# A stick-breaking and differential attention encoder on one core: the order of work in the first gate/up chunk, and two weights' rests moved to GpSimd

## The chip, the cores and the metric

The kernel runs on one core of a Trainium2 chip. The time is that of one execution on the device, in microseconds. A core has engines with a queue of instructions each, which run in order and wait for each other through semaphores: TensorE (PE in the profile, its weight loads PEld), VectorE (DVE), ScalarE (ACT), GpSimd (POOL) and SyncE (SP), whose queue here issues most of the transfers from the device's memory. GpSimd's queue issues transfers as well, here those that add to what they find (accumulating transfers). SBUF is the memory that the engines work in, PSUM the memory that TensorE writes its sums to.

## The reference

Two layers over 256 tokens of width 2048, all in float32. A layer is attention (eight stick-breaking heads, eight differential heads), a projection, a residual sum with a normalization, and a SwiGLU block with another:

```python
def swiglu(h, w_gate, w_up, w_down):
    return (jax.nn.silu(h @ w_gate) * (h @ w_up)) @ w_down

for l in range(DEPTH):                 # 2 layers
    h = rms_norm(x, pre_mix_norm[l])
    m = hybrid_mixer(h, l, ...)        # attention and the projection w_o
    x = x + rms_norm(m, post_mix_norm[l])
    h = rms_norm(x, pre_ffn_norm[l])
    f = swiglu(h, w_gate[l], w_up[l], w_down[l])   # 2048 -> 5632 -> 2048
    x = x + rms_norm(f, post_ffn_norm[l])
```

The change concerns the place where `x + rms_norm(m, ...)` ends and `h @ w_gate`, `h @ w_up` begin.

## The kernel before

**Products in three parts.** A float32 operand w is split into a rounded part `hi` (ScalarE copies w into TensorE's format) and a rest `lo` = w - hi (a subtraction on VectorE, 128x1024 elements for one weight pair). A product of x and w is then three products on TensorE: x's rest by hi, x's rounded part by hi, x's rounded part by lo. Each weight pair goes through four steps: its load (SP), `hi` (ScalarE), `lo` (VectorE), the products. `weights(i, ahead)` sees to it that the pairs up to i + ahead are prepared; `raw`, the buffer of a load, is one of four, so a load waits for the `lo` of the pair four places earlier (L241); `hi` and `lo` have six buffers each.

**Chunks.** The gate and up products run over chunks of 512 columns (`c`), each over eight pairs of 128 rows (`kp`). A pair is either done by `eight` (L1245: 24 products of 128x512, for two tokens' halves, gate and up), or by `seven` (L1127 to L1129: 21 products in place of 24), which needs sums: token sums `f` and `s`, split into `sh` and `sl` (`pair_sums`, `token_sums`, L1361, L1134 to L1145), and weight sums G and T. T is loaded (L257), then GpSimd's queue adds half of the gate weight to it with an accumulating transfer (L258), and `mixed_weights` makes from G and T the pieces `hi`, `lo` (L281), T's difference (L290), G's sum with it (L291) and their splits `Th`, `Tl` (L279, L281). In the first chunk the order of the pairs is `FIRST_ORDER` = 0, 1, 3, 2, 7, 4, 6, 5: four pairs (`first` to `fourth`) ahead of the loop, then 7 by `eight`, 4 and 6 by `seven`, 5 by `eight`. In layer 1 their weights have the numbers 128/129, 130/131, 132/133, 134/135, 136/137, 138/139, 140/141 and 142/143; in layer 2 each is 392 higher.

**The stretch around the change** (from L1252). x is updated column group by column group: `rescaled` (L647, VectorE, x + r * mg), then `turned_x` transposes four 128x128 blocks on TensorE (L502), `rounded_x` makes x's rounded part on ScalarE (L508) and `rest_of_x` its rest on VectorE (L516); `columns` is the last two together. TensorE meanwhile works on the pairs whose columns are there already. A part of this stretch is written out by hand (`tc.manual_schedule` for ScalarE, VectorE and TensorE): in it the instructions of an engine stand in the order of the source. Behind it the order is a scheduler's, which `tc.issue_after` can hold back: the instruction is placed after the named one. `rounded_next` gives the next pair's `hi` and returns a function that issues its `lo`; its argument is the engine, VectorE if none is given (L334). Before, the pairs 132 and 133 use it in this stretch; 134 to 137 come through `feed` (L317), as `eight(..., third, ...)` has the usual look-ahead of four.

**The squares.** The norm in front of the SwiGLU needs the mean of x squared: `inv_rms` (L542) has eight squares of 128x512 on ScalarE in each layer, then small steps on VectorE (L545, L485, L495, L496) and ScalarE (L483, L484). Its result is first used at the end of the chunk (L1413).

**Helped rests.** In later chunks two of the gate weights' rests are made by GpSimd (L310), one of them held back until the chunk before has its last seven-product pair's products.

Of the kernel before, what the change touches and what calls it, by code (L numbers as in the profile page):

```python
# [13 lines left out]
ALU = mybir.AluOpType  # L14
# [7 lines left out]
NT = S // P  # L22
# [22 lines left out]
FIRST_ORDER = (0, 1, 3, 2, 7, 4, 6, 5)  # L45
# [7 lines left out]
AFTER = mybir.DependencyInfo(mybir.DependencyClass.Sync, mybir.DependencyReason.DATA)  # L53
# [114 lines left out]
def kernel(  # L168
# [15 lines left out]
    nc = tc.nc  # L184
# [23 lines left out]
    for lay in plan:  # L208
        for c in range(1, FF // CW):
            for n in (1, 2):  # L210
                helped[lay["gate"][c, gate_order(c)[n]]] = n == 1
    newest_seven = [None]

    ready = {}
    raws, loads = [], []
# [47 lines left out]
    def mixed_weights(i):  # L263

        g, u = raws[i - 1], raws[i]
        hi = wpool.tile([P, 2, CW], F32R, tag="hi", bufs=6, name=f"hi{i}")
        lo = wpool.tile([P, 2, CW], F32R, tag="lo", bufs=6, name=f"lo{i}")
        if i in own:
            th = wpool.tile([P, 2, CW], F32R, tag="hi", bufs=6, name=f"Th{i}")
            tl = wpool.tile([P, 2, CW], F32R, tag="lo", bufs=6, name=f"Tl{i}")  # L270
            th2 = mix_pool[0].tile([P, 2 * (S + P)], F32R, tag="ah", bufs=1, name=f"T2h{i}")[:, 0:CW]
            tl2 = mix_pool[0].tile([P, 2 * (S + P)], F32R, tag="al", bufs=1, name=f"T2l{i}")[:, 0:CW]
        else:
            th = mix_pool[0].tile([P, 3, CW], F32R, tag="Th", bufs=1 if i in plain else 2, name=f"Th{i}")
            tl = mix_pool[0].tile([P, 3, CW], F32R, tag="Tl", bufs=1 if i in plain else 2, name=f"Tl{i}")
            th2, tl2 = th[:, 2, :], tl[:, 2, :]

        def split(h, l, w):
            nc.scalar.activation(h, w, AF.Copy)  # L279
            with in_row(i):  # L280
                newest_rest[i] = nc.vector.tensor_tensor(out=l, in0=w, in1=h.bitcast(F32), op=ALU.subtract)  # L281

        if i in plain or i in own:
            with after_rests():
                nc.vector.tensor_tensor(out=u[:, 0, :], in0=g[:, 0, :], in1=u[:, 0, :], op=ALU.add)
        split(hi, lo, u)
        t1, b22 = ((hi[:, k, :], lo[:, k, :]) for k in range(2))
        t3, t4 = ((th[:, k, :], tl[:, k, :]) for k in range(2))
        t2 = u[:, 1, :]
        nc.vector.tensor_tensor(out=t2, in0=t2, in1=u[:, 0, :], op=ALU.subtract)  # L290
        nc.vector.tensor_tensor(out=g, in0=g, in1=t2.unsqueeze(1).to_broadcast([P, 2, CW]), op=ALU.add)  # L291
        split(th2, tl2, t2)
        split(th[:, 0:2, :], tl[:, 0:2, :], g)
        t2 = th2, tl2
        return {"b22": b22, "t1": t1, "t2": t2, "t3": t3, "t4": t4}

# [25 lines left out]
    def rounded_next():  # L322

        i = fed[0]
        fetch(i + 1)
        raw = raws[i]
        hi = wpool.tile([P, 2, CW], F32R, tag="hi", bufs=6, name=f"hi{i}")
        nc.scalar.activation(hi, raw, AF.Copy)
        lo = wpool.tile([P, 2, CW], F32R, tag="lo", bufs=6, name=f"lo{i}")
        ready[i] = (hi, lo)  # L330
        fed[0] += 1

        def rest(eng=nc.vector):
            r = eng.tensor_tensor(out=lo, in0=raw, in1=hi.bitcast(F32), op=ALU.subtract)  # L334
            if eng is nc.vector:
                rests.append(r)
            return r

        return rest
# [304 lines left out]

    def rescaled(mg, t, c, r):
        sl = x_part(t, c * CW, CW)
        nc.vector.scalar_tensor_tensor(out=sl, in0=mg[t, c // 2][:, c % 2, :], scalar=r, in1=sl, op0=ALU.mult, op1=ALU.add)  # L647

    def rescale(mg, ssm, t, nm, then=None, newest=None):
        halves = newest is not None  # L650
# [527 lines left out]
    for l in range(L):  # L1178
# [73 lines left out]
        with tc.manual_schedule(engines=by_hand):  # L1252
# [41 lines left out]
            root = root_of(ssm, 1, nm)  # L1294
            next(root)
            next(root)
            rests_next.append(rounded_next())
            gain(2, 1)
            r.append(next(root))
            rescaled(mg, 1, 0, r[1])  # L1300
            pb.append(turned_x(1, 0))
            eight(first_banks, 0, second, (0,), False, False, (1,), 0)
            gain(3, 1)
            columns(pb[1], 1, 0)
            rescaled(mg, 0, 1, r[0])
            eight(first_banks, 0, first, (1,), True, False, ahead=0)
            pb.append(turned_x(0, 1))
            rounded_x(pb[2], 0, 1, g0, xT)
            rescaled(mg, 1, 1, r[1])
            rests_next.pop(0)()  # L1310
            rests_next.append(rounded_next())
            rest_of_x(pb[2], 0, 1, g0, xT)
            eight(first_banks, 0, second, (1,), False, False, (0,), 0)
            pb.append(turned_x(1, 1))
            rounded_x(pb[3], 1, 1, g0, xT)
            rests_next.pop(0)()
            eight(first_banks, 0, second, (1,), False, False, (1,), 0)
# [53 lines left out]
        for c in range(FF // CW):  # L1371
# [2 lines left out]
            order = gate_order(c)[0 if c else 4 :]  # L1374
            extra = None
            for n, kp in enumerate(order, 0 if c else 2):
                if (c, n) == (0, 2):
                    rs = [inv_rms(t, pool, f"ffn{l}", behind=newest) for t in range(NT)]
                if n == 1 and c in AWAY_AT:
                    put_away(f"ffn{l}", AWAY_AT.index(c))  # L1380
                for formed in FORM_AT.get((c, n), ()):
                    with after_rests():
                        pair_sums(formed)
                if c and n == 7:
                    start(turned(c - 1), 4)
                if kp not in mine:
                    eight(banks, c, kp, range(NT), kp == 0, kp == order[-1])
                    continue
                if kp == mine[0]:
                    extra = four_banks(c % 2, [f"{q}_{l}_{c}" for q in ("p1", "p6", "p7", "q5")])  # L1390
                seven(banks, extra, c, kp, kp == mine[0], kp == mine[-1])
                if kp == mine[-1]:
                    w = [pool.tile([P, CW], F32, tag="t2", name=f"w{j}_{l}_{c}") for j in range(4)]
                    end = shared_part(extra, w)
                    second = plan[l]["up"][c + 1, gate_order(c + 1)[1]] if c < LAST else None
                    if second in sevens:
                        follows[second] = end
                    else:
                        held[:] = end, 2 if second is None else 1
# [184 lines left out]
```

## Time and profile before

| | us |
|---|---|
| median of three runs | 2189.24 |
| lowest and highest of them | 2188.32, 2189.37 |
| the profiled execution | 2184.17 |
| its span (first to last instruction) | 2182.5 |

A timeline row of the profile has the start in us from the span's start, the duration in us of a group of equal neighbours, the engine, the line of the source, the operation, what it writes and reads (buffer numbers left out), the shape and the count; in brackets the idle time of the engine before it and what ended that. SPq is SyncE's queue of transfers. Instructions of VectorE and ScalarE that follow each other overlap by some 0.1 us, so a group is shorter than its durations' sum. In layer 1 the stretch lies at 386 to 464 us, in layer 2 some 1086 us later.

### The profile page before, as it was taken

Reading aid. Unit: us, or ns where it says so; the run is one execution under the profiler, and the core shown is the slowest. Engines: PE = TensorE matmul, PEld = TensorE weight load, DVE = VectorE, ACT = ScalarE, POOL = GpSimd, SP = SyncE. Lnnn points to the kernel's source line nnn. Section 1 sums busy time; section 2 is a strip of 40 time slices with the busy share of each in tenths; the row PEclk is TensorE's granted clock in tenths of the full one; section 3 lists DMA queues with packets and bytes.
Section 4 is the critical chain, followed back from the end, with each engine's and each line's share of the span. In section 5 each row is a group of like instructions: output and inputs, shape, how many; then the busy total and the mean of one; then the engine's idle time right before and its main releaser. Section 6 shows DMA issues by size and latency. Waiting matters only on the chain.

```text
span 2182.5 us, 28761 instructions
## 1 busy us (share of the span) xinstructions
PE 2165.1 (99%) x9944; PEld 1781.2 (82%) x9944; DVE 1920.9 (88%) x2657; ACT 1403.0 (64%) x2089; POOL 252.3 (12%) x243
## 2 busy tenths in 40 slices
PE   9999999999999999999999999999999999999998
PEld 7888888778888888888878888887888888888886
DVE  7888658899999999999878886588999999999997
ACT  7666665756666666666665666657666666676664
POOL 1100000021222220000010000000312212200000
PEclk9999999999999999999999999999999999999999
DMA  9544554488887767767464445545887877767672
GB/s 326 196 160 174 193 189 173 150 282 262 242 258 230 235 227 241 228 227 252 147 241 174 180 172 188 194 155 172 282 259 239 266 221 238 234 222 242 204 270 97
DMA packets 140850, 471.48 MB, mean 216 GB/s; under 512 B 16016, under 2 KB 17040, under 8 KB 140192
## 3 DMA queue, kind: packets, MB, share of 16 engines
q1 hardware_dynamic: 121952, 436.03, 55.3%
q0 software_dynamic: 18176, 33.07, 8.9%
q8 instruction: 78, 1.28, 0.2%
q10 hardware_dynamic: 576, 0.54, 0.1%
q14 instruction: 68, 0.56, 0.1%
HBM read 461.19 MB, written 8.39 MB: 215 GB/s over the span
## 4 chain that ended last, share of the span: by engine, by line
PE 92%; DVE 4%; ACT 2%; issue 1%; DMA 1%; DVEq 0%; SPq 0%; ACTq 0%
PE c L1245 18%; PE in L1127 7%; PE in L1129 7%; PE in L1128 7%; PE dn L1466 4%; PE dn L1465 4%; PE dn L1468 4%; PE p L1128 3%; PE p L1129 3%; PE c L1129 3%; PE c L1128 3%; PE c L1127 3%; PE p L1127 3%; PE o L599 2%; PE o L601 2%; PE o L600 2%
## 5 line engine op out<-in xcount | busy, mean ns | idle before, releaser
L317 DVE TENSOR_TENSOR lo<-raw,hi 128x1024 fp32r<-128x1024 f32 x456 | 546.2, 1220 | 99.2 <-ACT hi L307 98.1
L307 ACT ACTIVATE hi<-raw 128x1024 fp32r<-128x1024 f32 x478 | 488.5, 1053 | 96.0 <-DMA raw<-in_weights_in_turn_dram 46.0
L1245 PE MATMUL c<-hi,xF 128*128 128x512 f32 x1280 | 349.2, 392 | 0.9 <-DVE xF L516 0.5
L1245 PEld LDWEIGHTS c<-hi,xF 128*128 128x128 f32 x1280 | 238.0, 188 | 50.5 <-DVE xF L516 1.3
L258 POOL DMA_DIRECT2D T<-in_weights_in_turn_dram x126 | 111.3, 883 | 1376.9 <-DMA T<-in_weights_in_turn_dram 380.1
L1245 PE MATMUL c<-lo,xF 128*128 128x512 f32 x640 | 198.8, 390 | 0.0
L279 ACT ACTIVATE Th<-G 128x1024 fp32r<-128x1024 f32 x126 | 133.1, 1056 | 79.7 <-DVE G L291 78.8
L281 DVE TENSOR_TENSOR Tl<-G,Th 128x1024 fp32r<-128x1024 f32 x126 | 153.9, 1222 | 10.1 <-ACT Th L279 10.1
L1465 PE MATMUL dn<-hi,jh 128*128 128x512 f32 x416 | 162.0, 389 | 0.0
L1466 PE MATMUL dn<-lo,jh 128*128 128x512 f32 x416 | 161.8, 389 | 0.0
L307 ACT ACTIVATE hi<-G 128x1024 fp32r<-128x1024 f32 x126 | 133.3, 1058 | 43.5 <-DMA G<-in_weights_in_turn_dram 27.0
L281 DVE TENSOR_TENSOR lo<-T,hi 128x1024 fp32r<-128x1024 f32 x126 | 158.3, 1256 | 0.2 <-ACT hi L279 0.2
L291 DVE TENSOR_TENSOR G<-G,T 128x1024 f32<-128x1024 f32 x126 | 153.5, 1218 | 1.7
L279 ACT ACTIVATE Th<-T 128x512 fp32r<-128x512 f32 x126 | 79.7, 632 | 101.7 <-DVE T L290 98.3
L1245 PEld LDWEIGHTS c<-lo,xF 128*128 128x128 f32 x640 | 119.8, 188 | 25.7 <-DVE lo L317 0.7
L279 ACT ACTIVATE hi<-T 128x1024 fp32r<-128x1024 f32 x126 | 132.2, 1050 | 11.6 <-PE c L1129 9.5
L317 DVE TENSOR_TENSOR lo<-G,hi 128x1024 fp32r<-128x1024 f32 x108 | 131.6, 1219 | 7.9 <-ACT hi L307 7.8
L1127 PE MATMUL in<-hi,xT 128*128 128x512 f32 x328 | 131.0, 401 | 0.7 <-ACT hi L932 0.7
L1127 PE MATMUL in<-hi,xI 128*128 128x512 f32 x328 | 131.2, 401 | 0.0
L1128 PE MATMUL in<-lo,xI 128*128 128x512 f32 x328 | 128.0, 390 | 0.3 <-DVE lo L317 0.3
L1468 PE MATMUL dn<-hi,jl 128*128 128x512 f32 x416 | 128.0, 389 | 0.0
L1129 PE MATMUL in<-hi,xI 128*128 128x512 f32 x328 | 128.0, 391 | 0.0
(487 smaller groups left out, 4971.9 us busy)
## 6 DMA issues: line engine op xcount, KB each, us to landing
raw<-in_weights_in_turn_dram SPq DMA_DIRECT2D x490, 512.0 KB, 4.6
T<-in_weights_in_turn_dram SPq DMA_DIRECT2D x126, 512.0 KB, 5.4
G<-in_weights_in_turn_dram SPq DMA_DIRECT2D x126, 512.0 KB, 5.1
T<-in_weights_in_turn_dram POOLq DMA_DIRECT2D x126, 256.0 KB, 6.0
GU<-in_weights_in_turn_dram SPq DMA_DIRECT2D x32, 512.0 KB, 6.3
V<-in_weights_in_turn_dram SPq DMA_DIRECT2D x8, 512.0 KB, 3.7
away_ffn<-x SPq DMA_DIRECT2D x8, 512.0 KB, 7.9
xd<-away_ffn SPq DMA_DIRECT2D x8, 512.0 KB, 9.6
```

The lines of the kernel that those rows point to most:

```text
L279: nc.scalar.activation(h, w, AF.Copy)
L281: newest_rest[i] = nc.vector.tensor_tensor(out=l, in0=w, in1=h.bitcast(F32), op=ALU.subtract)
L291: nc.vector.tensor_tensor(out=g, in0=g, in1=t2.unsqueeze(1).to_broadcast([P, 2, CW]), op=ALU.add)
L307: nc.scalar.activation(hi, raw, AF.Copy)
L317: rest = nc.vector.tensor_tensor(out=lo, in0=raw, in1=hi.bitcast(F32), op=ALU.subtract)
L1127: nc.tensor.matmul(a, sh, hi, start=first, stop=False, skip_group_check=open_sums[0])
L1128: nc.tensor.matmul(a, sh, lo, start=False, stop=False, skip_group_check=open_sums[0])
L1129: return nc.tensor.matmul(a, sl, hi, start=False, stop=last, skip_group_check=open_sums[0])
L1245: nc.tensor.matmul(a, stat[part], w[j][:, kk, :], start=first and kk + n == 0, stop=last and kk == 1 and n == 2)
L1465: nc.tensor.matmul(accs[c, t], sh, hi[:, kk, :], start=first, stop=False, skip_group_check=open_sums[0])
L1466: nc.tensor.matmul(accs[c, t], sh, lo[:, kk, :], start=False, stop=False, skip_group_check=open_sums[0])
L1468: nc.tensor.matmul(accs[c, t], sl, hi[:, kk, :], start=False, stop=last, skip_group_check=open_sums[0])
```

## The change

It has six parts, the same for both layers.

- In the stretch by hand, the update of column group 1 of the first tokens (`rescaled(mg, 0, 1, r[0])`) moves ahead of `columns(pb[1], 1, 0)`, and the next weight's `hi` (132) behind them.
- The transposes `turned_x(0, 1)` and `turned_x(1, 1)` move six products earlier each on TensorE, and with `rest` 133 ahead of `rounded_x(pb[3], ...)`, the roundings and rests behind them.
- `third` is issued with a look-ahead of 2, so `feed` prepares only 134 and 135. The rests of 136 and 137 are issued by `rounded_next()(nc.gpsimd)` on GpSimd, the last update of x (`whole`) being what they wait for. On GpSimd's queue they stand ahead of the accumulating transfers to T 139 and T 141. The loads of 144 and 145 take the buffers of 136 and 137; in SP's queue they now stand behind the loads of T 139, T 141, G 138 and G 140.
- The four last updates of x (column groups 3 and 2) come first, then the transposes, roundings and rests; on TensorE the sixteen transposes stand in a row at the end of the third pair instead of between the fourth's products.
- `inv_rms` is called one pair later. On ScalarE its squares stand behind the first `sh`, the `hi` of 138 to 141 and among the second `sh` and `Th`, instead of ahead of all of these.
- `first_of_two`: behind the first seven-product pair's last rest (139) come the second pair's rests (140, 141) on VectorE; before, they stood among the first's.

```diff
@@ beside newest_seven
+    first_of_two = {lay["up"][0, FIRST_ORDER[5]] for lay in plan}
@@ mixed_weights
         split(th[:, 0:2, :], tl[:, 0:2, :], g)
+        if i in first_of_two:
+            follows[i + 2] = newest_rest[i]
+            held[:] = newest_rest[i], 1
@@ rescaled
-        nc.vector.scalar_tensor_tensor(out=sl, ...)
+        return nc.vector.scalar_tensor_tensor(out=sl, ...)
@@ the stretch written out by hand
             next(root)
             next(root)
-            rests_next.append(rounded_next())
             gain(2, 1)
...
             gain(3, 1)
+            rescaled(mg, 0, 1, r[0])
             columns(pb[1], 1, 0)
-            rescaled(mg, 0, 1, r[0])
-            eight(first_banks, 0, first, (1,), True, False, ahead=0)
+            rests_next.append(rounded_next())
+            eight(first_banks, 0, first, (1,), True, False, (0,), 0)
             pb.append(turned_x(0, 1))
+            eight(first_banks, 0, first, (1,), True, False, (1,), 0)
             rounded_x(pb[2], 0, 1, g0, xT)
...
             rest_of_x(pb[2], 0, 1, g0, xT)
-            eight(first_banks, 0, second, (1,), False, False, (0,), 0)
             pb.append(turned_x(1, 1))
+            eight(first_banks, 0, second, (1,), False, False, ahead=0)
+            rests_next.pop(0)()
             rounded_x(pb[3], 1, 1, g0, xT)
-            rests_next.pop(0)()
-            eight(first_banks, 0, second, (1,), False, False, (1,), 0)
             newest = rest_of_x(pb[3], 1, 1, g0, xT)
-        eight(first_banks, 0, third, range(NT), False, False)
+        eight(first_banks, 0, third, range(NT), False, False, ahead=2)
         for cg in (3, 2):
             for t in range(NT):
                 with tc.issue_after(newest.ins):
-                    rescaled(mg, t, cg, r[t])
+                    whole = rescaled(mg, t, cg, r[t])
+        for cg in (3, 2):
+            for t in range(NT):
                 columns(turned_x(t, cg), t, cg)
+            rest = rounded_next()(nc.gpsimd)
+            tc.add_manual_dep(rest.ins, whole.ins.name, AFTER, reason="the shared port")
         eight(first_banks, 0, fourth, range(NT), False, False, ahead=2)
@@ the loop over chunks
-                if (c, n) == (0, 2):
+                if (c, n) == (0, 3):
                     rs = [inv_rms(t, pool, f"ffn{l}", behind=newest) for t in range(NT)]
```

More of the change, by code (lines that the diff above doesn't have):

```diff
@@ L646, in rescaled @@
         sl = x_part(t, c * CW, CW)
-        nc.vector.scalar_tensor_tensor(out=sl, in0=mg[t, c // 2][:, c % 2, :], scalar=r, in1=sl, op0=ALU.mult, op1=ALU.add)
+        return nc.vector.scalar_tensor_tensor(out=sl, in0=mg[t, c // 2][:, c % 2, :], scalar=r, in1=sl, op0=ALU.mult, op1=ALU.add)
     def rescale(mg, ssm, t, nm, then=None, newest=None):
```

## The prediction

> **What bounds the kernel now.** The page came first.
>
> ```profile
> span 2182.5 us, 28761 instructions
> PE 2165.1 (99%) x9944; PEld 1781.2 (82%) x9944; DVE 1920.9 (88%) x2657; ACT 1403.0 (64%) x2089; POOL 252.3 (12%) x243
> ```
>
> TensorE sets the end, so only an instant at which it stands still can be won. The change touches the first gate/up chunk of each layer, so the busy time of its stretches was asked next, for layer 1 (columns: the stretch, then busy time and count by engine, granted clock, DMA share, GB/s).
>
> ```profile
> 392.00:423.50 31.50, 31.27 (x152) 25.54 (x151) 24.79 (x64) 20.98 (x59) 1.76 (x2) 1.00 0.65 228
> 423.50:442.00 18.50, 16.45 (x65) 11.16 (x65) 18.50 (x26) 12.70 (x17) 0.38 (x1) 1.00 0.29 102
> 442.00:464.40 22.40, 22.40 (x100) 18.55 (x99) 20.82 (x34) 14.32 (x16) 8.23 (x5) 1.00 0.94 328
> ```
>
> Before 423.5 and after 442 TensorE runs; between them VectorE is busy 18.50 of 18.50 us and TensorE is not. The price of this comes from TensorE's own rows.
>
> ```profile
> 398.88 1.20 PE L1245 MATMUL c<-hi,xF 128*128 128x512 f32 x4 [0.23 <-DVE xF L516]
> ...
> 405.40 1.09 PE L1245 MATMUL c<-hi,xF 128*128 128x512 f32 x4
> ...
> 412.22 0.40 PE L1245 MATMUL c<-hi,xF 128*128 128x512 f32 x1
> 412.46 0.60 PE L502 MATMUL xT_ps<-ident,x 128*128 128x128 f32 x4
> 412.82 0.48 PE L1245 MATMUL c<-hi,xF 128*128 128x512 f32 x1
> 413.13 0.60 PE L502 MATMUL xT_ps<-ident,x 128*128 128x128 f32 x4
> ...
> 423.56 0.44 PE L1127 MATMUL p<-hi,xF 128*128 128x512 f32 x1
> ...
> 425.35 0.50 PE L1127 MATMUL q<-hi,sh 128*128 128x512 f32 x1 [1.12 <-ACT sh L1144]
> ...
> 464.46 0.39 PE L1127 MATMUL p<-hi,xF 128*128 128x512 f32 x1
> ```
>
> The third pair of weights begins at 405.40, and 30 products later it is 412.22: the pace is 0.227 us a product. From the first product of a seven-product pair (423.56) to the first one of the next chunk (464.46) the code has 2 x 21 + 24 + 4 x 24 = 162 products: 36.8 us of 40.9, so 4.1 us are lost. The largest single loss is the wait for sh before 425.35. In layer 2 that wait is 1.5 instead of 1.1:
>
> ```profile
> PE q L1127 <- ACT sh L1144: 1.5, 1, 1.5
> ```
>
> Who is late there is told by ScalarE's rows.
>
> ```profile
> 413.10 4.25 ACT L508 ACTIVATE xF<-xT_ps,gains 128x128 fp32r<-128x128 f32 x16 [3.06 <-PE xT_ps L502]
> 417.11 0.75 ACT L542 ACTIVATE junk_ffn<-x 128x512 f32<-128x512 f32 x1
> ...
> 422.30 1.14 ACT L307 ACTIVATE hi<-G 128x1024 fp32r<-128x1024 f32 x1
> 423.63 1.06 ACT L279 ACTIVATE hi<-T 128x1024 fp32r<-128x1024 f32 x1
> 424.69 0.61 ACT L1144 ACTIVATE sh<-s 128x512 fp32r<-128x512 f32 x1
> ```
>
> Eight squares (L542) fill 417.11 to 422.30; T's rounding at 423.63 starts 4.67 us after GpSimd issued T's accumulation, and sh stands behind it:
>
> ```profile
> 418.96 0.89 POOL L258 DMA_DIRECT2D T<-in_weights_in_turn_dram  x1 [270.00 <-DVE xF L516]
> ...
> 411.79 0.90 SPq L257 DMA_DIRECT2D T<-in_weights_in_turn_dram  x2
> ```
>
> And VectorE's rows, with the three gaps that the change closes (2.02, 1.50, and 1.31 with 1.15):
>
> ```profile
> 398.47 1.12 DVE L516 SCALAR_TENSOR_TENSOR xF<-xT_ps,gains,xF 128x128 fp32r<-128x128 f32 x4 [2.02 <-ACT xF L508]
> ...
> 400.84 1.22 DVE L334 TENSOR_TENSOR lo<-raw,hi 128x1024 fp32r<-128x1024 f32 x1
> 403.56 1.12 DVE L516 SCALAR_TENSOR_TENSOR xF<-xT_ps,gains,xF 128x128 fp32r<-128x128 f32 x4 [1.50 <-ACT xF L508]
> ...
> 406.77 4.62 DVE L317 TENSOR_TENSOR lo<-raw,hi 128x1024 fp32r<-128x1024 f32 x4
> 411.31 2.73 DVE L647 SCALAR_TENSOR_TENSOR x<-mg_o,tot_o,x 128x512 f32<-128x512 f32 x4
> 414.28 4.23 DVE L516 SCALAR_TENSOR_TENSOR xF<-xT_ps,gains,xF 128x128 fp32r<-128x128 f32 x16 [0.24 <-ACT xF L508]
> 419.82 0.16 DVE L545 TENSOR_REDUCE ssx_ffn<-ssp_ffn 128x1 f32<-128x4 f32 x1 [1.31 <-ACT junk_ffn L542]
> ...
> 421.31 0.22 DVE L495 SCALAR_TENSOR_TENSOR rsq_ffn<-rs_ffn,rsq_ffn 128x1 f32<-128x1 f32 x1 [1.15 <-ACT rs_ffn L484]
> 421.64 0.76 DVE L1361 TENSOR_TENSOR f<-xF 128x256 f32<-128x256 f32 x2
> ...
> 424.55 1.22 DVE L317 TENSOR_TENSOR lo<-G,hi 128x1024 fp32r<-128x1024 f32 x1
> ...
> 439.91 2.35 DVE L317 TENSOR_TENSOR lo<-raw,hi 128x1024 fp32r<-128x1024 f32 x2
> ```
>
> **The change part by part** (layer 1's clock). Paces from these rows: a 1024-wide rest 1.135 us (four from 406.77 to 411.31), a 512-wide update of x 0.67, an x rest 0.26, a 1024-wide rounding on ScalarE about 0.95.
>
> First gap: one update of x moves into the 2.02 us, so lo of weight 132 starts at 400.2 instead of 400.84 (its rounding, moved behind x's, runs in ScalarE's idle time from 398.4). TensorE's wait just before 398.88 hangs on x's rests at 398.47, which do not move: no gain there.
>
> Second gap: the transposes stand 6 products earlier, 6 x 0.227 = 1.36 us, so x's rests start at 402.2 instead of 403.56, and the rest of 134 at 405.45 instead of 406.77.
>
> Two rests leave VectorE: 2 x 1.135 = 2.27 us. The last four updates of x run from 405.45 + 2.27 = 407.7 to 410.4 instead of 411.31 to 414.04. TensorE did not wait for any of this: its third pair (24 products from 405.40) ends at 410.9 in either order. The 16 transposes now stand in a row there instead of spread from 412.46; between single products each block of four costs 0.09 in the product behind it (412.82 to 413.13 is 0.31 instead of 0.227), and three of four such costs go: -0.27. ScalarE rounds x from 411.5 instead of 413.10, VectorE's x rests run 412.6 to 416.9 instead of 414.28 to 418.5.
>
> Third gap: with the squares behind sh in ScalarE's queue, VectorE goes straight on to f at 416.9 instead of 421.64, and lo of 138 starts at 419.6 instead of 424.55. VectorE is 4.9 us early. That is more than the 4.1 us that TensorE loses; but it is not what ends last any more.
>
> The two subtractions on GpSimd, by its rows:
>
> ```profile
> 481.13 2.40 POOL L310 TENSOR_TENSOR lo<-raw,hi 128x1024 fp32r<-128x1024 f32 x1 [13.34 <-DVE lo L317]
> L310 POOL TENSOR_TENSOR lo<-raw,hi x22: 2396/2446/3213, 441.6 to 1895.5; 128x1024 fp32r<-128x1024 f32 x22
> ```
>
> From 2.40 undisturbed to 3.21. They start with the last update of x, 410.6, and end at 413.0 and 415.4 (417.0 at 3.2). Their products are wanted at 417.7: covered by pair four, with 2.3 us in hand; without that cover the excess is TensorE's. Queued behind them on GpSimd are T's two accumulations. T's own loads go out at 408.2 instead of 411.79 (the two loads that wait for GpSimd now stand behind T and G on SP), and before they were there by 418.96, 7.2 us after their issue, so now by 415.4. So the first accumulation leaves at 415.4 instead of 418.96, 3.55 us earlier. Its landing is bounded by two rows:
>
> ```profile
> T<-in_weights_in_turn_dram POOLq DMA_DIRECT2D x1, 256.0 KB, 3.5
> T<-in_weights_in_turn_dram POOLq DMA_DIRECT2D x126, 256.0 KB, 6.0
> ```
>
> 3.5 us with little else under way, 6.0 as the median. I take this place's own 4.67, since two to three loads are under way beside it in both orders: T lands at 420.1 instead of 423.6.
>
> From there ScalarE carries the chain, in its new order: T's rounding, G's next one, sh (done 422.6), T's next, two squares (0.62 each), the second sh (425.3), three squares to 427.1, Th's third at 427.7, a square, Th's pair to 429.4. VectorE waits in it: lo of 139 423.4 to 424.6, the second sl 425.3, T's difference to 426.5, Tl of the pair not before 429.4 to 430.5, then lo of 140 (431.65), lo of 141 (432.8) and 8.6 us more without a wait, to 441.4 instead of 442.3. TensorE arrives at 423.3, runs 12 products to 426.0 and then waits 1.7 us for Th, 0.4 and 0.3 for Tl, 0.1 for lo of 140, 0.8 for the second Th pair (436.1), each with 0.1 to refill: 3.8 us against 4.1. Layer 1: -0.27 - 0.35 = -0.6. In layer 2 the accumulation lands 0.35 later now (its sh wait is that much longer), and afterwards it hangs on GpSimd's queue as in layer 1: -0.95. Sum -1.6 us. The second pair's rests behind the first's are in these orders already and move no instruction's size.
>
> The profiled execution took 2184.17 us, its span 2182.5, so 1.7 lie around it; it becomes 2182.6. The median of the runs is 2189.24, 5.1 above it; on that median I forecast 2187.6.
>
> **The rivals.** Until 429.4 every step hangs on T's landing, so a microsecond there is worth about a microsecond a layer; at 420.75 nothing is won.
>
> A. T lands at the unloaded price, 418.9: another -1.2 a layer, -4.0 in all, 2185.2. For it: two loads that ran ahead of T now run behind. Against: these are just then being fetched. If all of 4.1 + 0.27 went twice, it would be 2180.5; T cannot land that early.
>
> B. The accumulation takes the median 6.0: +1.3 a layer on the forecast, +1.1 in all, 2190.3; with a microsecond more, 2192.3. For it: the loads of 144 and 145 are issued at 413 and 415.4, beside it. [...]
>
> C. The other side: GpSimd and x's rests hinder each other. If the second subtraction comes to its turn only when the rests end (416.9), it ends at 419.3, the accumulation lands at 424.0, 3.9 later than in the forecast: +7.8 - 1.6 = +6.2, 2195.4. It decides from an issue later than 416.1 on. Against it:
>
> ```profile
> 488.21 2.40 POOL L310 TENSOR_TENSOR lo<-G,hi 128x1024 fp32r<-128x1024 f32 x1 [0.27 <-ACT hi L307]
> 488.51 1.40 DVE L1418 SCALAR_TENSOR_TENSOR act<-c,rs_ffn,w 128x512 f32<-128x512 f32 x2
> 489.82 1.86 DVE L281 TENSOR_TENSOR lo<-T,hi 128x1024 fp32r<-128x1024 f32 x1
> ```
>
> Two operations of the rests' kind (one operand in PSUM, one in SBUF, a column) ran beside a 2.40 subtraction at 0.74 each; only the one with both operands in SBUF took 1.86 instead of 1.22. But sixteen short ones in a row beside GpSimd are not in this trace. [...]
>
> D. The change does not do what it says: the gaps close and VectorE's time reappears in front of 423.5, nothing else moves: 2189.2. Little speaks for it, as ScalarE's order changes in any case.
>
> **How the numbers follow.** Forecast 0.41 (own range 2186.6 to 2188.6, T's landing 0.5 to either side in each layer), A 0.24, B 0.18, C 0.15, D 0.02. 0.2%, about what a measurement can tell here from no change, is 4.4 us. Faster by more: 0.15, the better part of A, which stands 0.4 us from that bound. Slower by more: C's 0.15 and 0.05 of B. Within: 0.65. The range, 2184.5 to 2194.0, leaves out C and A's far end.
>
> **What would show it.** Right: x's last rest near 416.9 and f right behind it; two GpSimd subtractions near 2.4 us that end at 415.4; T's first rounding near 420.1; no sh wait on TensorE, a Th wait of 1 to 2 us in its place; ScalarE without idle time from there to 429; the next chunk's seven-product pair at 463.8 instead of 464.46. Wrong: subtractions over 3 us, an accumulation over 6 us, x's rests slower than 0.26, or waits in any chunk but the first.

## The result, and the profile after

| | before | changed |
|---|---|---|
| median, us | 2189.01 | 2194.97 |
| lowest and highest of 11 runs | 2186.65, 2191.32 | 2193.19, 2196.98 |
| the profiled execution | 2184.17 | 2196.98 |

The ratio is 1.0025 (95% interval 1.0017 to 1.0033): some 6 us slower, outside the predicted range of 2184.5 to 2194.0. The two profiled executions lie 12.8 us apart, more than the medians, as that of before was 4.8 us faster than its own median and that of the changed kernel 2.0 us slower. So profiles serve here for places and mechanisms, and medians for prices. A second set of runs of the changed kernel (below) gave 1.0026 (1.0015 to 1.0037).

The page of the changed kernel, its span and the busy times:

```profile
span 2195.2 us, 28776 instructions
PE 2174.1 (99%) x9944; PEld 1784.0 (81%) x9944; DVE 1921.1 (88%) x2653; ACT 1399.2 (64%) x2089; POOL 270.7 (12%) x247
```

TensorE, with as many matmuls as before, is busy 9.0 us longer: some of its products ran slower. The timeline of TensorE around the stretch, its ends first:

```profile
399.88 1.20 PE L1249 MATMUL c<-hi,xF 128*128 128x512 f32 x4 [0.23 <-DVE xF L520]
...
427.21 0.50 PE L1131 MATMUL q<-hi,sh 128*128 128x512 f32 x1 [1.18 <-ACT sh L1148]
429.28 0.50 PE L1132 MATMUL q<-lo,sh 128*128 128x512 f32 x1 [1.56 <-DVE lo L282]
432.26 0.80 PE L1131 MATMUL p<-Th,sh 128*128 128x512 f32 x1 [0.80 <-ACT Th L280]
432.86 0.63 PE L1131 MATMUL p<-hi,xF 128*128 128x512 f32 x1
433.28 0.63 PE L1132 MATMUL p<-Tl,sh 128*128 128x512 f32 x1
...
468.68 0.39 PE L1131 MATMUL p<-hi,xF 128*128 128x512 f32 x1
```

The changed kernel runs about 1 us late from its start (399.88 for 398.88), which is no doing of the change; 1.00 is taken off below to compare with layer 1's clock of before. From the wait at 399.88 to the next chunk's seven-product pair it needs 68.80 us; the same two rows of before (398.88 and 464.46) are 65.58 apart. So 3.22 us are lost here, where the forecast won 0.6; in layer 2, 2.1. Three waits in a row stand where there was one large one, and behind them the products are 0.42 us apart (432.86 to 433.28), not 0.227. The stretches of this time say why (columns as in the prediction, the granted clock behind the counts):

```profile
424.00:427.00 3.00, 2.04 (x9) 1.34 (x8) 0.00 (x0) 2.36 (x3) 0.00 (x0) 1.00 0.13 25
427.00:430.00 3.00, 1.23 (x4) 0.78 (x5) 2.14 (x4) 3.00 (x8) 0.00 (x0) 0.94 0.01 3
430.00:433.00 3.00, 2.21 (x6) 1.16 (x4) 3.00 (x6) 3.00 (x11) 0.00 (x0) 0.50 0.00 0
433.00:436.00 3.00, 3.00 (x9) 2.34 (x8) 2.12 (x4) 3.00 (x8) 0.00 (x0) 0.50 0.00 0
436.00:439.00 3.00, 3.00 (x14) 2.46 (x13) 3.00 (x7) 3.00 (x5) 0.00 (x0) 0.92 0.00 0
```

VectorE, which was always busy here before, does nothing from 424 to 427, and the granted clock of TensorE is 0.50 from 430 to 436. (The 0.94 and 0.92 beside these rows put the ends of that fall near 429.7 and 436.5.) Who is late is told by GpSimd's and SyncE's rows and by ScalarE's:

```profile
411.63 4.74 POOL L338 TENSOR_TENSOR lo<-raw,hi 128x1024 fp32r<-128x1024 f32 x2 [261.52 <-DVE x L651]
416.32 1.78 POOL L259 DMA_DIRECT2D T<-in_weights_in_turn_dram  x2
...
414.04 2.69 SPq L242 DMA_DIRECT2D raw<-in_weights_in_turn_dram  x2
...
418.22 1.06 ACT L311 ACTIVATE hi<-G 128x1024 fp32r<-128x1024 f32 x1 [1.49 <-DVE f L1369]
424.64 1.06 ACT L280 ACTIVATE hi<-T 128x1024 fp32r<-128x1024 f32 x1 [5.35 <-DMA T<-in_weights_in_turn_dram]
425.60 1.04 ACT L311 ACTIVATE hi<-G 128x1024 fp32r<-128x1024 f32 x1
426.55 0.61 ACT L1148 ACTIVATE sh<-s 128x512 fp32r<-128x512 f32 x1
...
431.60 0.61 ACT L280 ACTIVATE Th<-T 128x512 fp32r<-128x512 f32 x1
```

GpSimd issues T's first accumulation at 416.32, in before's clock 415.32, as predicted. But ScalarE then waits 5.35 us for T: it landed at 424.56 (the trace's record of the transfer), 8.24 us after its issue, where the forecast had 4.67. In before's clock that is 423.6, the same time as before: the 3.6 us won on GpSimd's queue are gone. And what ScalarE used to do in this time, the squares, now stands behind T. The two `raw` loads at 414.04 are those of 144 and 145.

### The profile page after: what moved, and what is told of

It is laid out like the page before. It is cut to its first block, busy times and chain, and to the rows that moved or that the text cites. A ratio compares the mean times of both kernels' runs of the same rounds, so it can differ in the third digit from the quotient of the medians.

```text
span 2195.2 us, 28776 instructions
## 1 busy us (share of the span) xinstructions
PE 2174.1 (99%) x9944; PEld 1784.0 (81%) x9944; DVE 1921.1 (88%) x2653; ACT 1399.2 (64%) x2089; POOL 270.7 (12%) x247
## 4 chain that ended last, share of the span: by engine, by line
PE 83%; DVE 9%; issue 3%; DMA 2%; ACT 2%; DVEq 0%; SPq 0%; ACTq 0%
PE c L1249 15%; PE in L1131 7%; PE in L1133 6%; PE in L1132 6%; PE dn L1473 4%; PE dn L1474 4%; PE dn L1476 4%; PE o L603 2%; PE o L605 2%; PE o L604 2%; DVE Tl L282 2%; PE p L1132 2%; PE p L1131 2%; PE c L1131 2%; PE p L1133 2%
## 5 line engine op out<-in xcount | busy, mean ns | idle before, releaser
L311 ACT ACTIVATE hi<-raw 128x1024 fp32r<-128x1024 f32 x474 | 483.2, 1052 | 89.9 <-DMA raw<-in_weights_in_turn_dram 39.8
L1131 PE MATMUL in<-hi,xI 128*128 128x512 f32 x328 | 131.1, 401 | 0.0
L1132 PE MATMUL in<-lo,xT 128*128 128x512 f32 x328 | 127.8, 391 | 0.5 <-DVE lo L321 0.3
```

The costliest lines, as they stand in the source:

```text
L1131: nc.tensor.matmul(a, sh, hi, start=first, stop=False, skip_group_check=open_sums[0])
L1132: nc.tensor.matmul(a, sh, lo, start=False, stop=False, skip_group_check=open_sums[0])
```

## The experiments

Theory 1: the loads of 144 and 145, which the change issues around the accumulation, stretch it; T is late for that, and the rest follows. Its rivals: the squares' new place (theory 2), the fall of the granted clock (theory 3), the ordering `first_of_two`, the subtractions on GpSimd. Each run is compared with runs of the kernel before on the same chip, whose medians lay between 2187.25 and 2187.94 (2189.01 in the first set); the runs come from several chips, so rows are compared with each other by their differences from before. "Accumulations" is the median of the two from issue to landing in layers 1 and 2; it is 5.0 and 5.0 in before. "Stretch" is the time between the two rows used above, both layers together, against before.

| run | median minus before, us | 95% interval of the ratio | accumulations, us | stretch, us |
|---|---|---|---|---|
| changed, first set | +5.96 | 1.0017 to 1.0033 | 8.5, 8.1 | +5.3 |
| e13: changed, again | +5.03 | 1.0015 to 1.0037 | 8.1, 7.6 | +5.3 |
| e1: squares back | +1.10 | 0.9997 to 1.0015 | 7.8, 7.8 | -0.6 |
| e5: without `first_of_two` | +1.85 | 0.9996 to 1.0014 | 7.4, 8.4 | +4.3 |
| e10: 145 held | +1.82 | 0.9999 to 1.0017 | 6.3, 6.1 | +2.1 |
| e4: 144 and 145 held | -1.04 | 0.9988 to 1.0005 | 4.6, 5.1 | -2.0 |
| e7: held, squares back | -4.15 | 0.9975 to 0.9993 | 5.2, 5.0 | -5.0 |
| e11, e17: held, without `first_of_two` | -5.46, -5.06 | 0.9965 to 0.9984, 0.9969 to 0.9987 | 4.9, 5.1; 5.1, 5.1 | -3.4, -3.2 |
| e14, e18: held, squares back, without `first_of_two` | -7.05, -5.89 | 0.9954 to 0.9979, 0.9960 to 0.9982 | 6.1, 5.1; 4.8, 4.9 | -5.1, -5.7 |
| e2: rests on VectorE | -2.10 | 0.9982 to 0.9999 | 4.7, 4.8 | -1.6 |
| e12: rests on VectorE, without `first_of_two` | -1.93 | 0.9982 to 1.0000 | 5.0, 5.2 | -2.8 |
| e16: the three gaps alone | -3.91 | 0.9975 to 0.9992 | 5.9, 5.5 | -0.6 |
| e8: rests on VectorE, squares later still | +0.47 | 0.9994 to 1.0012 | 4.9, 5.6 | +2.9 |
| e3: before with the squares moved | +1.02 | 0.9997 to 1.0015 | 5.0, 5.8 | +0.3 |
| e15: before with `first_of_two` | +4.93 | 1.0018 to 1.0039 | 5.5, 4.9 | +2.6 |
| e6: changed, TensorE's waits filled | +7.68 | 1.0022 to 1.0047 | 8.5, 7.6 | +9.8 |

**The loads held (e4).** Both are held until T 141 has been rounded once:

```diff
+    late_load = {lay[n][1, 0]: lay["up"][0, FIRST_ORDER[6]] for lay in plan for n in ("gate", "up")}
+    first_hi = {}
...
             with not_ahead(i) if mixing else nullcontext():
                 loads.append(nc.sync.dma_start(raw, stream[i]))
+            if i in late_load:
+                tc.add_manual_dep(loads[-1].ins, first_hi[late_load[i]].ins.name, AFTER, reason="the accumulations")
...
-            nc.scalar.activation(h, w, AF.Copy)
+            first_hi.setdefault(i, nc.scalar.activation(h, w, AF.Copy))
```

> The changed kernel, with the loads of 144 and 145 (in layer 2: 536 and 537) held until T 141 has been rounded for the first time, so that they do not run beside the accumulations. Theory 1: the first accumulation, issued at about 416.3, takes 4.7 to 5.5 us instead of 8.24, T lands near 421.5, sh near 424 and the waits fall below those of before: 2186.5 to 2189, the blind forecast's own place. Theory 2: T may land earlier, but the squares still hold sh and Th back: 2193 or more. If the landing is held by something else (the two loads of G, the accumulation's own traffic): it still takes about 8 us and nothing changes, 2195. Against the gain: 144 and 145 land some 6 us later, near 430, still long before the next chunk's start at 464.

Measured -1.04 us against before, 6 to 7 below the changed kernel. The accumulation, issued at 415.55, is down to 3.8 us in layer 1 and 5.0 in layer 2. ScalarE's row for T, two microseconds earlier than expected:

```profile
419.41 1.06 ACT L284 ACTIVATE hi<-T 128x1024 fp32r<-128x1024 f32 x1 [1.39 <-DMA T<-in_weights_in_turn_dram]
```

Theory 2 wanted 2193 or more with the squares where the change puts them; it was 2186.78. Theory 1 stands, as a size: the same orders with T early have no loss.

**One load held (e10).** The diff of e4 with `("up",)` for `("gate", "up")`.

> The changed kernel with only the load of 145 (537 in layer 2) held until T 141 has been rounded; 144 still runs beside T's accumulation. Dose: with both beside it the accumulation took 8.24 us, with neither 3.79. Theory 1 in its plain form (the transfers share the bandwidth, so each half megabyte beside it costs its share): in between, 5.5 to 7 us, and 2188 to 2192. If 144 alone, which is issued ahead of it, holds it back: 8 us and 2194 or more. If 145 alone does: 4 us and 2187.

The plain form of theory 1 fits: 6.3 and 6.1 us, +1.82 us. The step from no load to one is not clear of the noise, though: accumulations without either load beside them go up to 6.2 us (e14, layer 1), and the intervals of e4 and e10 overlap. How the time is lost is seen in the transfers of the 4 us from the issue on. The view of transfers, by queue (q1 is SyncE's, q0 GpSimd's; packets, MB, share of the 16 DMA engines), for 418.96 to 422.96 of the kernel before:

```profile
q1 hardware_dynamic: 231, 0.81, 50.7%
q0 software_dynamic: 173, 0.33, 48.8%
```

For 415.55 to 419.55 of e4 (neither load beside it):

```profile
q0 software_dynamic: 199, 0.37, 56.5%
q1 hardware_dynamic: 171, 0.59, 36.2%
```

For 417.07 to 421.07 of e10 (one load):

```profile
q1 hardware_dynamic: 347, 1.24, 76.6%
q0 software_dynamic: 59, 0.12, 24.8%
```

And for 416.32 to 420.32 and then 420.32 to 422.32 of the changed kernel (both):

```profile
q1 hardware_dynamic: 398, 1.43, 93.1%
...
q1 hardware_dynamic: 102, 0.37, 51.5%
q0 software_dynamic: 91, 0.18, 50.0%
```

GpSimd's queue has no row at all in the first 4.0 us of the changed kernel: not one packet of the accumulation moved, while SyncE's queue kept the engines 93% busy. Stepped through in quarters of a microsecond, its first packet comes within 1.75 us of the issue in before and in e4, 2.5 in e10, and 4.5 in the changed kernel and in e13. Layer 2 has 2.0 in before and 4.0 in the changed kernel. Only then do the two queues share by halves (51.5% and 50.0% from 420.32 to 422.32). So the longer accumulation of layer 1 is a late start of some 2.75 us and about 0.85 more behind it, where the load of 145 is still under way (it lands at 424.87).

**The squares (e1, e3).** e1 is the changed kernel, e3 the kernel before, each with the one line turned round:

```diff
-                if (c, n) == (0, 3):
+                if (c, n) == (0, 2):
```

> The changed kernel, with the norm's eight squares (inv_rms) called where they stood before, so that ScalarE has them ahead of T's rounding again; all else stays changed. Theory 1 (the loads of 144 and 145 run beside T's accumulation and stretch it from 4.67 to 8.24 us, so T lands no earlier; the squares are then late work behind it): the accumulation still takes about 8 us and T lands near 424.6, but sh follows T's rounding at once and Th comes about 2 us earlier (near 429.5 instead of 431.6); the waits fall to about those of before, 2189 to 2191 us. Theory 2 (the squares' place alone makes the loss): 2189 or less, whatever T does; it differs from theory 1 only in the run that moves the squares alone. Theory 3 (short waits in a row lower TensorE's granted clock to 0.5 for some 6 us): the clock stays at 1.00 here if fewer waits stand together, which gives back up to 2.8 us a layer. If instead the rests on GpSimd or the order of the second pair make the loss, the time stays near 2195.

> The kernel before, with only the squares moved one pair later, as in the change. Theory 2 (the squares' place is the loss): 2194 to 2196, as much as the whole change, with sh's wait and Th's together over 2 us on TensorE. Theory 1 (late T): T lands at 423.6 as before, since no load is moved, and the squares behind it delay Th by about 2 us a layer: 2191 to 2194. [...] If the squares do no harm: 2189.

e1 gave back 4 to 5 us although the accumulation took 7.8 us: ScalarE's wait for T is filled with squares again. Its 2188.92 is just under what theory 1 expected and fits theory 2 as well. e3 tells them apart: it lost 1.02 us, within its interval, where theory 2 asked for the whole loss; theory 1's own number for it, 2191 to 2194, was wrong too. There sh stands ahead of T's rounding on ScalarE and the squares harm little. So the squares' place is not the cause alone, but it has a price of its own beside the changed orders: 4 to 5 us with T late (e1), 3.1 with T early (e4 against e7).

**The rests on VectorE (e2).**

```diff
-        eight(first_banks, 0, third, range(NT), False, False, ahead=2)
+        eight(first_banks, 0, third, range(NT), False, False)
...
-            rest = rounded_next()(nc.gpsimd)
-            tc.add_manual_dep(rest.ins, whole.ins.name, AFTER, reason="the shared port")
```

> The changed kernel, with the rests of 136 and 137 on VectorE as before (no subtraction on GpSimd here; the loads of 144 and 145 then go out ahead of T again). Theory 1: nothing runs beside the accumulation but G's loads, so it takes about 4.7 us again; but T's own load goes out later, so T lands at about 423.6 as in the kernel before, with the squares behind it: Th stays late (431 or so) and the time is 2193 to 2196. If the subtractions on GpSimd themselves were the loss: about 2189. If the squares are the whole loss: 2195.

Here theory 1's number was wrong: 2185.72, not 2193 to 2196. The accumulation took 4.7 us as expected and T landed at 422.9, but ScalarE's order had changed too: both sh now stood ahead of T's rounding, and TensorE had no wait for sh. That the loss goes with the GpSimd rests agrees with theory 1, as without them the loads of 144 and 145 go out ahead of T; the subtractions themselves took 4.74 us for two, undisturbed. By itself e2 cannot tell the subtractions from the loads, as it takes both away; e4 does, as it keeps the subtractions on GpSimd and has no loss.

**The clock (e6).** Spare products on TensorE, in the three waits of the first seven-product pair:

```diff
+    def spare(count, bank, job):
+        for _ in range(count):
+            with tc.issue_after(newest_seven[0].ins):
+                newest_seven[0] = nc.tensor.matmul(bank, job[1][0], job[2][0], start=True, stop=True, skip_group_check=True)
```

> The changed kernel with spare products on TensorE (their sums are overwritten) in the three waits of the first seven-product pair: 5, 7 and 6 of them in layer 1, 2, 7 and 6 in layer 2, fitted to the waits that the trace shows, so that TensorE has work there and nothing else moves in this chunk. Theory 3 (the clock fell to 0.50 because TensorE stood still): the granted clock stays at 1.00 behind them and the 14 products that were 0.427 us apart are 0.227 apart. That is up to 2.8 us a layer; but VectorE's Tl of the pair ends near 435.2 in either case, which leaves only about 1 us a layer to be had: 2190 to 2193.5. If the clock fell for another reason: 0.50 again, and 2195 or more.

The view of stretches of e6:

```profile
427.00:430.00 3.00, 2.89 (x12) 1.80 (x11) 2.03 (x3) 3.00 (x8) 0.00 (x0) 1.00 0.01 3
430.00:433.00 3.00, 2.84 (x12) 1.88 (x10) 2.70 (x5) 3.00 (x10) 0.00 (x0) 1.00 0.00 0
433.00:436.00 3.00, 1.73 (x5) 0.78 (x5) 2.11 (x4) 3.00 (x9) 0.00 (x0) 1.00 0.00 0
```

The clock stayed at 1.00, with TensorE busy for 2.89 of the 3.00 us from 427 to 430, where the changed kernel had 1.23 and a fall from 429.7 on: between these two runs the fall went with TensorE's lack of work. The time did not get better (2194.93, +7.68; 2190 to 2193.5 was expected), but the spare products also changed the order of the ones behind them: the second pair's, which used to stand between the first's, came after, and TensorE waited 1.20 us for the second Tl. So the price of the fall is not settled. At half pace ten products of layer 1 in the changed kernel came 0.427 instead of 0.227 us apart, which is 2.0 us and not the 2.8 of the expectation; and the product at 436.27, which ends this, needed a Tl that VectorE had at 435.2 (433.99 + 1.23), so that 1.1 us of it could have come back at most.

The clock fell in other runs too. In the profiles it was at 0.50 for 6.8 us in each layer of the changed kernel (from 429.7 and from 1521.9 us) and in layer 1 of e13 and e10, for 3.4 us in layer 1 of e5 and e15 (in e15 from 427.8 us), and for 3.4 us between 470 and 480 us in e1. In before it stayed at 1.00 until the last 4.1 us of the program, and in e2, e3, e4, e6, e8, e14 and e16 it was 1.00 from 424 to 442 us. Over the whole profiled execution its mean was 0.996 in the changed kernel and e13, 0.997 in e5, e10 and e15, 0.998 in e1, and 0.999 or 1.000 in all the others. So a part of what is lost in the runs with a fall may be the clock's; no run took the falls away and left the rest as it was.

**The second pair's order (e5, e15).** e5 takes the three lines of `first_of_two` out of the changed kernel; e15 puts them alone into the kernel before.

> The changed kernel without first_of_two: the second seven-product pair's rests may stand among the first's again on VectorE. If that ordering has a part in the loss, the time falls by a microsecond or more, to 2194 or less. If the late T is the cause, the accumulation still takes 7 to 8.5 us, T's rounding still starts near 424.6 and the time stays at 2194 to 2196.

> The kernel before with first_of_two alone. If the ordering costs something by itself: 2190 to 2193, some 4 us above the kernel before. If it costs only because T's late landing left TensorE without other products in its waits: the kernel before has T at 423.6 as well, but sh without a wait behind it, so 2187 to 2189.

Both went against theory 1, which had given the ordering nothing: e5 is some 3 to 4 us below the changed kernel with T about as late (1.2 us earlier in layer 1, 0.7 later in layer 2), and e15 loses 4.93 us with no other change and has a fall of the clock in its profile (3.4 us in layer 1). VectorE's timeline of e15 shows what the ordering does,

```profile
431.85 0.69 DVE L282 TENSOR_TENSOR Tl<-T,Th 128x512 fp32r<-128x512 f32 x1
433.69 1.23 DVE L282 TENSOR_TENSOR Tl<-G,Th 128x1024 fp32r<-128x1024 f32 x1 [1.16 <-ACT Th L280]
434.83 1.22 DVE L321 TENSOR_TENSOR lo<-G,hi 128x1024 fp32r<-128x1024 f32 x1
```

beside that of the kernel before:

```profile
429.02 1.22 DVE L317 TENSOR_TENSOR lo<-G,hi 128x1024 fp32r<-128x1024 f32 x1
430.16 1.22 DVE L291 TENSOR_TENSOR G<-G,T 128x1024 f32<-128x1024 f32 x1
431.29 0.68 DVE L281 TENSOR_TENSOR Tl<-T,Th 128x512 fp32r<-128x512 f32 x1
431.90 1.22 DVE L281 TENSOR_TENSOR lo<-T,hi 128x1024 fp32r<-128x1024 f32 x1
```

VectorE stands 1.16 us in front of the last Tl of the first pair, waiting for ScalarE, and the rest of G 140, ready long before, is queued behind it: 434.83 instead of 429.02 (0.85 us of that is e15's later start). Before, it filled the wait. In the next chunk TensorE then waits longer for Tl, in e15 between 470 and 480 us:

```profile
PE p L1132 <- DVE Tl L282: 2.2, 2, 1.5
```

Before waits 0.7 us for it there, once. That this wait follows from the later rest is argued from the order on VectorE and not shown by itself.

**Squares later still (e8).** e2 with `(0, 4)` for `(0, 3)`.

> The changed kernel with the two rests on VectorE and the squares one pair later still, behind the first pair's Th on ScalarE. With the rests on VectorE alone the time was 2185.7, and TensorE still waited for Th (0.39 and 0.46 us), Tl (0.70) and a rounding (0.80) that stood behind squares. If the squares' place makes these waits: they fall to under 1 us together and the time to 2183 to 2185. If T's landing makes them: 2185.7 again. Against a gain: the norm's result then comes some 3 us later, and the roundings of 142 and 143 may be late instead.

It was 2187.72, some 2.6 us worse than e2 against before, and fits neither expectation. The waits for Th and Tl did not go away (0.84 and 0.53 us more than the usual pace), and TensorE had a new one of 1.16 us at 445.94.

**Parts put together.** e13 is the changed kernel once more, e7 is e4 with the squares back, e11 and e17 are e4 without `first_of_two`, e12 is e2 without it, e14 and e18 are e7 without it, e16 is e12 with the squares back.

> The changed kernel itself once more, beside the others of this set. Theory 1: both loads beside the accumulation, so it takes 7 to 8.5 us again in both layers, T lands no earlier than before, and the time is some 6 us above the kernel before (2193 to 2196 where that one is at 2187 to 2189). If the first result came from a disturbance of that session, it falls to within 2 us of the kernel before. The many short waits in later chunks of the first profile (3.7 us in layer 1, 2.0 in layer 2) were not in the medians' sum: another profile should have 0 to 2 us of them.

> The changed kernel with the loads of 144 and 145 held and the squares back ahead of T's rounding. Theory 1 with the squares filling ScalarE's wait for T: T lands near 419.1 to 419.5, but the squares then end near 421 to 422 and stand in front of T's rounding, so T's early landing is not used: sh near 422 to 423, and 2186 to 2188. If the squares among sh and Th cost more than that: below 2185.

> The changed kernel with the loads of 144 and 145 held and without first_of_two. The ordering cost about 4 us where T was late (2189.1 without it). If it costs as much where T is early, the time falls to 2183 to 2185; if it cost only because TensorE had nothing else in its waits for the late T, it stays at 2186 to 2187.5, as with the loads held alone.

> The changed kernel with the two rests on VectorE and without first_of_two: what is left of the change is the three gaps and the squares. With the rests on VectorE alone it was 2185.7. If the ordering costs something in itself: 2183 to 2185. If it only mattered where T was late beside a ScalarE that waited for it: 2185 to 2187.

> The changed kernel with the loads of 144 and 145 held, the squares back and without first_of_two: what is left is the three gaps and the two rests on GpSimd. In six profiles with the squares moved and the later chunks (500 to 800 us) compared with the kernel before, TensorE lost 0.3 to 3.7 us there, in the two with the squares back 0.0. If that is real: 2180 to 2182, about a microsecond or two below the same kernel with the squares moved (2182.5). If not: 2182 to 2184.

> The changed kernel with the rests on VectorE, the squares back and without first_of_two: the three gaps alone. T lands about a microsecond earlier than before (422.5 with the rests on VectorE), the squares fill ScalarE's wait: 2185 to 2187. If the gaps are worth nothing: 2188.

> The version with the loads of 144 and 145 held and without first_of_two once more, beside the one that has the squares back as well: 2181.5 to 2183.5, 0.2 to 0.3% below the kernel before, if the first result holds.

> The fastest version so far (three gaps closed, the two rests on GpSimd, the loads of 144 and 145 held, the squares and the second pair's order as before) once more: 2180 to 2182, some 6 to 7.5 us below the kernel before, if its first result holds; above 2183.5 if that was luck.

e13 repeated the loss. Against my expectation e7 was better than 2186 (2183.79), and the ordering cost as much with T early (e11 against e4: 4.4 us) as with T late. e14 and e18 are the fastest: 0.3% below the kernel before, with both intervals below 1. Read as a ladder, each row adding one part and using the mean where a version ran twice:

| | median minus before, us | this step |
|---|---|---|
| the three gaps (e16) | -3.9 | -3.9 |
| and the rests on GpSimd, loads held (e14, e18) | -6.5 | -2.6 |
| and the squares moved (e11, e17) | -5.3 | +1.2 |
| and `first_of_two` (e4) | -1.0 | +4.2 |
| and the loads not held: the change | +5.5 | +6.5 |

A single step has an uncertainty of 2 to 3 us, so the rests on GpSimd (-2.6) and the squares (+1.2) are not settled by this ladder alone; but the loads come out at 6.5, 5.3 (e7 to e1) and about 7 (e11 and e17 to e5), the squares at 1.0 to 4.4 in five pairs (e1, e3, e7, e14 and e16 and their partners), the ordering at 4.9, 4.2, about 3.6 and 2.3, and at nothing only with the rests on VectorE and the squares moved (e2, e12).

## Why the prediction was wrong

**Up to T's issue it was right.** VectorE's timeline of the changed kernel:

```profile
401.18 1.22 DVE L338 TENSOR_TENSOR lo<-raw,hi 128x1024 fp32r<-128x1024 f32 x1
403.19 1.13 DVE L520 SCALAR_TENSOR_TENSOR xF<-xT_ps,gains,xF 128x128 fp32r<-128x128 f32 x4 [0.79 <-ACT xF L512]
...
408.67 2.73 DVE L651 SCALAR_TENSOR_TENSOR x<-mg_o,tot_o,x 128x512 f32<-128x512 f32 x4
413.66 4.24 DVE L520 SCALAR_TENSOR_TENSOR xF<-xT_ps,gains,xF 128x128 fp32r<-128x128 f32 x16 [2.26 <-ACT xF L512]
417.82 0.75 DVE L1369 TENSOR_TENSOR f<-xF 128x256 f32<-128x256 f32 x2
...
420.57 1.23 DVE L321 TENSOR_TENSOR lo<-G,hi 128x1024 fp32r<-128x1024 f32 x1
427.19 0.69 DVE L1149 TENSOR_TENSOR sl<-s,sh 128x512 fp32r<-128x512 f32 x1 [5.40 <-ACT sh L1148]
```

Less 1.00, the rest of 132 is at 400.2, x's second rests at 402.2, the last updates of x at 407.7, x's rests from 412.7, f at 416.8, lo of 138 at 419.6, and the accumulation at 415.3: all within 0.1 of the forecast's times. The last row is where it ends: 5.40 us of VectorE without work. The two subtractions took 2.37 us each, the second of them (414.0 to 416.4) beside x's rests, which kept their 0.26, so rival C is out.

**The step that failed** is "I take this place's own 4.67, since two to three loads are under way beside it in both orders". The term was mis-sized: it measured 8.24 us in layer 1 and 7.53 in layer 2 of the changed kernel's first profile, and 7.9 in layer 1 of e13. The count of loads was wrong. Counting those that are issued by then (0.5 us after it at the latest) and land after its issue, three of 512 KB each were beside it in before, in both layers: T 141 and the two of G. In the changed kernel there were five: the same three, as the whole group had moved with it, and those of 144 and 145, issued 2.3 us before it and in the same tenth of a microsecond. I had named these two, as the case for rival B, and bounded the price by 6.0, which is a median of 126 transfers and no end of a range: in that profile of before they run from 3.5 to 9.4 us. Of those that are not issued behind an unfinished one, the ten with five or more loads beside them took 7.2 to 9.4 us, all others 3.5 to 7.7, and the seventeen with three 4.3 to 7.3. So the profile of before had the price of five loads. Whether their bytes or their late issue makes it, the runs at this place do not separate, as both loads that were added were new. The prediction's own sign of being wrong, an accumulation over 6 us, came.

**With that term put right the forecast's sum comes out near:** the measured 8.24 and 7.53 in the place of 4.67 make -1.6 + 3.57 + 2.86 = +4.8 us, and +5.96 and +5.03 were measured. e4, with the same orders and neither of the two loads beside the accumulation, has -1.04 where -1.6 was forecast; its interval, some -2.6 to +1.1 us, holds the forecast, but also no gain at all. Its T lands at 419.1 in layer 1, a microsecond earlier than forecast. "A microsecond there is worth about a microsecond a layer" fits as well: from e4 to the changed kernel T's landing moves by 4.5 us in layer 1 (419.1 to 423.6) and the stretch by 4.7 (64.12 to 68.80 us), in layer 2 by 2.5 and 2.6.

**But the sum hid its parts.** "The second pair's rests behind the first's are in these orders already and move no instruction's size" is no error of the sum, which replayed these orders, but it left their price unseen: the ordering costs 2 to 5 us in four pairs of runs and nothing in one, the squares' move one to four, and the closed gaps with the rests on GpSimd and the two loads held win 6.5. That a bundle of such parts came near -1.6 with T early says little about any of them. The forecast replayed the final orders as one and never asked what each edit would do without the others. In the chunk's stretch the gaps alone show only -0.6 us (e16) of their 3.9; where the rest of it lies one profile of each kernel cannot show.

**Rivals.** B was the right mechanism, beyond its far end. Behind the accumulation's first packet the trace shows the two queues sharing the engines by halves (51.5% and 50.0% from 420.32 to 422.32); that does not give the 4.3 us (layer 1) and 3.9 us (layer 2) until that packet. D is out: every order moved as read. "No sh wait on TensorE" was wrong (1.18 us), as a consequence of T. Of "waits in any chunk but the first": products over 0.3 us apart cost the changed kernel's two profiles 3.9 and 2.3 us between 500 and 800 us, and before's one profile 0.6, as e1 and e7, with the squares back; as that profile of before lies 4.8 us under its median, it stays open whether they belong to the change.

**Not foreseen:** the granted clock of 0.50 after the waits.

## What to carry to other kernels

A transfer that sets the end is to be priced with all that is under way or issued beside it, counted in the order after the change, and a median of the same transfer elsewhere is no upper end; the longest of them, and what lies beside those, is in the same profile. Whoever moves work off one engine's queue should follow what its buffers release: here the rests on GpSimd freed two buffers just then, and the two loads that took them cost more than the rests saved; holding them for 8 to 10 us, in which nobody needed them, gave it back. Work without a deadline (the squares, a rest that is ready) belongs in front of a wait and not behind it, and each edit of a bundle deserves a run of its own, as a sum that comes out right may hide parts of both signs.

## What the runs showed of the hardware

At this place an accumulating transfer of 256 KB on GpSimd's queue had its first packet 1.7 and 1.8 us after its issue (layers 1 and 2 of before; within 1.75 in layer 1 of e4) with loads of SyncE's queue under way and no new one near it, within 2.5 (layer 1 of e10) with one load of 512 KB more, issued 2.3 us before, and 4.3 and 3.9 (layers 1 and 2 of the changed kernel; within 4.5 in layer 1 of e13) with a second one issued beside it; until then none of its packets moved, and SyncE's queue kept the engines 93% busy in the first 4.0 us (changed kernel, layer 1). For the ten accumulations in the profile of before that had five or more loads beside them and none of their own queue, it was 4.1 to 4.3 us. Why its first packet comes no earlier was not tried.

The granted clock of TensorE fell to 0.50 from 429.7 to 436.5 us in the changed kernel, after waits of 1.18 and 1.56 us with TensorE 41% busy between 427 and 430; in its layer 2 from 1521.9 to 1528.7, after waits of 0.47 and 1.56 us; and for 6.8 us in layer 1 of e13 again. With products in the waits (e6) it stayed at 1.00 from 424 to 442 us. The falls in layer 1 of e5 and e15 and the one of e1 lasted 3.4 us. Which wait or how little work sets off a fall was not shown.
